# MLP's first product in two halves of 512 moving columns, from the fourth piece on

## The chip, the cores and the metric

The kernel runs on one core of one Trainium2 chip. The metric is device time in microseconds, the median of several runs.

## The reference

Two layers over 256 tokens of width 1024. The first mixes by neighbourhood attention and latent attention, the second by dilated windows. Each layer ends in a squared-ReLU MLP with 4096 inner features. That MLP is what the change touches:

```python
def rms_norm(x, g):
    xf = x.astype(jnp.float32)
    y = xf * lax.rsqrt(jnp.mean(xf * xf, axis=-1, keepdims=True) + RMS_EPS)
    return (y * g.astype(jnp.float32)).astype(x.dtype)

def sq_relu_mlp(xn, w1, w2):
    return jnp.square(jax.nn.relu(xn @ w1)) @ w2

def reference(...):
    for layer in range(DEPTH):
        xn = rms_norm(x, norm_mix[layer])
        ...
        x = x + sq_relu_mlp(rms_norm(x, norm_mlp[layer]), mlp_w1[layer], mlp_w2[layer])
    return rms_norm(x, norm_final)
```

## The kernel before

Every product of float32 numbers is made of three products of fp32r numbers. A number is split into a high part, a cast by ScalarE (ACT), and a low part, number minus high part, by VectorE (DVE). `split` (lines 217 to 219) does it, and `mm3` (lines 221 to 224) issues the three matmuls: high by high, high by low, low by high. So weights `raw` that come from memory become `whi` and `wlo`, tokens become `xx` (both parts in one tile, `xT[:, k, 0]` high and `xT[:, k, 1]` low, which lie next to each other), and inner features `h` become `hh` and `hl`.

An MLP works in 16 pieces of 256 inner features. `up(j, pu)` makes piece j of the first product: for each half f of 128 features and each of 8 slices k of the width, three matmuls with 128 weight columns as the stationary and 256 tokens as the moving operand, into one PSUM bank of 512 columns, 256 for each half. Then ACT takes relu (line 386) and the square `h` (line 388). The second product uses seven block products in place of eight (`SEVEN`, after Strassen) for pieces 0 to 13: three subtractions on DVE (lines 393 to 395) make the operands from `h`, and `down(j, m)` issues 7 times three matmuls of 512 columns into banks `m`. Pieces 14 and 15 use eight plain block products, made at the end by `last`.

The order in the program is up(0), up(1), up(2), down(0), up(3), down(1), up(4), down(2) and so on to up(15), down(13). From up(3) on, `up` writes the bank `m["C22"]`, which no other product uses before `last("C22")`. I call up(j + 2) and the down(j) behind it a round. Banks of PSUM have the names `w` and `acc` in the profile; C22 is one of the four `w`.

Weights come on SyncE's DMA queue, 1 MB for a piece of w1 and 0.75 MB for three blocks of w2. For the seven products, sums of blocks of w2 are needed too: a base block is loaded into `sum` (line 140), copied by ACT (line 154), and two more blocks are added to it by an accumulating DMA that GpSimd issues (line 155). DVE adds further sums (`raw` line 189, `every` line 190), and ACT and DVE split them into `sumh` and `suml`. `weight()` hands out the next weight tiles and, ahead of them, issues loads and splits. There are three buffers for `whi`/`wlo`, four for `raw`, three for `sum`, two for `sumh`/`suml`, one for `h`.

A scheduler sets the order of instructions on each engine from their dependencies and priorities; `tc.high_priority` moves what stands in it forward. Each engine then works through its list in that order.

In the second MLP (`finish`), `beside` is `tokens_first`: while down(2), down(4), down(6) and down(8) run, PE turns a quarter of the tokens (four transposes, line 502) in the bank C22, and ACT copies it out (line 503).

The odd layer's `qk_steps` (lines 955, 956, 962, 963) already multiplies both parts of the tokens as one moving operand of 512 columns: the high weights by both parts into 512 columns of a bank, then the low weights by the high parts into columns 256 to 511. ACT copies the upper half of the bank to `low`, and DVE adds it to the lower half.

Of the kernel before, what the change touches and what calls it, by code (L numbers as in the profile page):

```python
# [22 lines left out]
ALU = mybir.AluOpType  # L23
# [3 lines left out]
P = 128  # L27
D = 1024
KT = D // P
T = 256  # L30
# [19 lines left out]
def trunk(ctx, tc, a, out):  # L50
# [9 lines left out]
    def scratch(shape, name):  # L60

        n = int(np.prod(shape))
        v = work.tile([P, 512], F32, tag="scratch", name=name, bufs=12)[:, :n]
        if len(shape) == 2:
            v = v.rearrange("p (a b) -> p a b", b=shape[1])
        return v
# [298 lines left out]

    EIGHT = {"P2": ((1, 0), (0, 1)), "Q3": ((1, 3), (0, 2)), "C22": ((3, 3), (2, 2)), "Q4": ((3, 0), (2, 1))}

    def mlp(mp, xT, s, apart=(), beside=lambda j, p: None):

        hs = {}
        quarters = [act.tile([P, KT // 2, T], F32R, tag="quarter", name="hh", bufs=4) for _ in range(3)]

        def up(j, pu):
            w = weight()

            ranges = [range(4), range(4, 6), range(6, 8)] if j == 0 else [range(8)]
            for ks in ranges:
                for f in range(2):  # L380
                    for k in ks:
                        c = slice(k * 256 + f * P, k * 256 + f * P + P)
                        mm3(pu[:, (1 - f) * T:(2 - f) * T], w[0][:, c], w[1][:, c], xT[:, k, 0, :], xT[:, k, 1, :],
                            k == 0 and (f == 0 or j > 0), k == KT - 1 and (f == 1 or j > 0))
            r = scratch([512], "relu")
            nc.scalar.activation(r, pu, AF.Relu)
            h = mp.tile([P, 8, P], F32, tag="h", name="h", bufs=1)
            nc.scalar.activation(h[:, 4:8, :].rearrange("p (t f) n -> p f t n", f=2), r.rearrange("p (f t n) -> p f t n", f=2, t=2), AF.Square)
            hh = quarters[j % 3].rearrange("p a (b n) -> p (a b) n", n=P)
            hl = mp.tile([P, 7, P], F32R, tag="hl", name="hl", bufs=3)  # L390
            hs[j] = hh, hl
            if j < 14:
                nc.vector.tensor_tensor(h[:, 2:4, :], h[:, 7:8, :].broadcast_to([P, 2, P]), h[:, 5:7, :], op=ALU.subtract)
                nc.vector.tensor_tensor(h[:, 1, :], h[:, 5, :], h[:, 3, :], op=ALU.subtract)
                nc.vector.tensor_tensor(h[:, 0, :], h[:, 4, :], h[:, 1, :], op=ALU.subtract)  # L395
                split(hh[:, 0:7, :], hl, h[:, 0:7, :])
            else:
                split(hh[:, 0:4, :], hl[:, 0:4, :], h[:, 4:8, :])

        def down(j, m):  # L400
            wh, wl = weight()
            hh, hl = hs[j]
            first = j == 0
            for n, i, b in SEVEN:
                end = j == 13 and (n not in EIGHT or n in apart)
                mm3(m[n], hh[:, i, :], hl[:, i, :], wh[b], wl[b], first, end)
                if n == "Q3":
                    beside(j, m["C22"])

        for j in range(3):  # L410
            up(j, bank("w"))
        inv = inverse_columns(s)
        m = {n: bank("w" if n in ("P1", "P2", "Q6", "C22") else "acc") for n in ("P1", "P2", "Q6", "C22", "Q7", "Q5", "Q3", "Q4")}
        for j in range(14):
            if j:
                up(j + 2, m["C22"])
            down(j, m)
        tail = {j: weight() for j in (14, 15)}

        def last(n, o=None, c=slice(0, BLK)):  # L420
            o = m[n] if o is None else o
            new = n == "C22" or n in apart
            for j, w in tail.items():
                for i, (at, b) in enumerate(EIGHT[n]):
                    wh, wl = (z[:, b * BLK + c.start:b * BLK + c.stop] for z in w)
                    mm3(o, hs[j][0][:, at, :], hs[j][1][:, at, :], wh, wl, new and (j, i) == (14, 0), (j, i) == (15, 1))

        return m, last, inv
# [56 lines left out]
    def finish(mp, xT, s):  # L485

        state["pool"] = mp
        HALF = [slice(0, 512), slice(512, D)]
        xt = []
        v = {}  # L490

        def tokens_first(j, pt):

            if j % 2 == 0 and 2 <= j < 10:
                t, h = divmod(j // 2 - 1, 2)
                if not xt:

                    spare = act.tile([P, KT // 2, T], F32R, tag="quarter", name="xt0", bufs=4)
                    xt.extend((spare.bitcast(F32).rearrange("p k n -> p (k n)"), mp.tile([P, D], F32, name="xt1")))
                v[t, h] = xt[t][:, HALF[h]]  # L500
                for k in range(4):
                    nc.tensor.transpose(pt[:, k * P:(k + 1) * P], x[:, 4 * h + k, tok(t)], ident)
                nc.scalar.copy(v[t, h], pt)

        m, last, inv = mlp(mp, xT, s, ("Q4",), tokens_first)
        i0, i1 = (column(inv, t) for t in range(NT))
        g = [scratch([512], "gain") for _ in HALF]
        for h, cs in enumerate(HALF):
            nc.sync.dma_start(g[h], a["norm_final"][cs].partition_broadcast(P))

        def square_sum(z, o):
            nc.scalar.activation(scratch([z.shape[-1]], "junk"), z, AF.Square, scale=D ** -0.5, accum_out=o)

        def sub(o, y, z, op=ALU.subtract):
            nc.vector.tensor_tensor(o, y, z, op=op)
            return o

        sc = lambda n: scratch([512], n)
        last("P2")
        p = sc("p")  # L520
        nc.scalar.copy(p, m["P1"])
        onto_tokens(v[0, 0], p, i0, v[0, 0])
        both = sub(sc("both"), m["Q6"], p)
        c12 = sub(p, m["Q5"], both, ALU.add)
        c21 = sub(both, m["Q7"], both, ALU.add)
        onto_tokens(v[0, 1], c12, i0, v[0, 1])
        onto_tokens(v[0, 0], m["P2"], i0, v[0, 0])
        c22 = sub(sc("c22"), m["Q5"], c21, ALU.add)
        last("Q3")
        c21 = sub(c21, m["Q4"], c21)  # L530
        onto_tokens(v[1, 1], c22, i1, v[1, 1])
        onto_tokens(v[0, 1], m["Q3"], i0, v[0, 1])
        onto_tokens(v[1, 0], c21, i1, v[1, 0])
        last("C22")


        ss = work.tile([P, 4], F32, tag="ssf", name="ss")
        for h in range(2):
            square_sum(v[0, h], ss[:, h:h + 1])
            sub(v[0, h], v[0, h], g[h], ALU.mult)  # L540
        nc.vector.tensor_scalar(ss[:, 2:3], ss[:, 0:1], ss[:, 1:2], EPS, ALU.add, ALU.add)
        r = rsqrt(ss[:, 2:3], "x")
        onto_tokens(v[1, 1], m["C22"], i1, v[1, 1])
        for h, cs in enumerate(HALF):
            y = sc("y")
            nc.scalar.activation(y, v[0, h], AF.Copy, scale=r)
            nc.sync.dma_start(out[0:P, cs], y)


        ss = work.tile([P, 4], F32, tag="ssf", name="ss")  # L550
        xg = [sc("xg") for _ in range(2)]
        square_sum(v[1, 1], ss[:, 0:1])
        sub(xg[1], v[1, 1], g[1], ALU.mult)
        for i, c in enumerate((slice(0, 256), slice(256, 512))):
            o = bank("w")[:, 0:256]
            last("Q4", o, c)
            z = v[1, 0][:, c]
            onto_tokens(z, o, i1, z)
            if i == 0:
                square_sum(z, ss[:, 1:2])  # L560
                sub(xg[0][:, c], z, g[0][:, c], ALU.mult)
            else:
                nc.vector.tensor_scalar(ss[:, 2:3], ss[:, 0:1], ss[:, 1:2], EPS, ALU.add, ALU.add)
                nc.vector.tensor_tensor_reduce(out=scratch([256], "junk"), in0=z, in1=z, op0=ALU.mult, op1=ALU.add,
                                               scale=1.0 / D, scalar=ss[:, 2:3], accum_out=ss[:, 3:4])
        r = rsqrt(ss[:, 3:4], "x")

        parts_of = [(xg[h][:, 256 * i:256 * i + 256], out[P:T, 512 * h + 256 * i:512 * h + 256 * i + 256]) for h in (1, 0) for i in range(2)]
        nc.scalar.activation(parts_of[0][0], parts_of[0][0], AF.Copy, scale=r)
        for z, _ in parts_of[1:3]:  # L570
            nc.vector.tensor_scalar(z, z, r, None, ALU.mult)
        nc.vector.scalar_tensor_tensor(parts_of[3][0], v[1, 0][:, 256:512], r, g[0][:, 256:512], ALU.mult, ALU.mult)
        for n, (z, o) in enumerate(parts_of):
            (nc.scalar, nc.sync, nc.sync, nc.scalar)[n].dma_start(o, z)
# [609 lines left out]
```

## Time and profile before

| | |
|---|---|
| median of 3 runs | 731.53 us (731.29 to 731.69) |
| profiled execution: time / span | 731.99 us / 730.2 us |
| granted TensorE clock, mean | 0.997 |
| first MLP, first relu to last relu | 122.4 to 269.7 us of the span |
| second MLP, first relu to last relu | 558.1 to 708.8 us of the span |
| copies like `low` (128x256, ACT, line 962) | 0.366 us, 42 of them |
| adds like `z` (128x256, DVE, line 963) | 0.416 us, 42 of them |

The profile gives for each instruction its start in the span, its duration, its engine, its line and its tiles (out<-in). PE is TensorE's matmuls and PEld its weight loads, DVE is VectorE, ACT ScalarE, POOL GpSimd, SP SyncE. Matmuls overlap: a duration is longer than the distance to the next start.

### The profile page before, as it was taken

What the parts mean: (1) busy time and instruction counts of PE and PEld (TensorE: products, weight loads), DVE (VectorE), ACT (ScalarE), POOL (GpSimd) and SP (SyncE); (2) the same over time, 40 slices, a digit from 0 to 9 for tenths busy, and PEclk for the clock granted to TensorE, in tenths of its full rate; (3) what the DMA queues carried; (4) which work ended last, traced back from release to release, by engine and by line L of the source; (5) the groups of instructions that cost most, each with busy time, mean ns of one, the idle gap of its engine ahead of it and who ended that gap; (6) DMA issues with size and microseconds to landing.
All of it is one profiled execution on the core that took longest, in us unless ns stands there. A gap on an engine that the chain in (4) does not pass through costs nothing.

```text
span 730.2 us, 13797 instructions
## 1 busy us (share of the span) xinstructions
PE 721.5 (99%) x5234; PEld 661.0 (91%) x5234; DVE 614.0 (84%) x1179; ACT 531.5 (73%) x1001; POOL 40.7 (6%) x51
## 2 busy tenths in 40 slices
PE   9999999999999999999999999999999999999996
PEld 6998999999999998989899899998999999999995
DVE  5887859989999959889777888778759999989857
ACT  6778977876877856877676766867658788767752
POOL 0100011110111000000000000000002110011000
PEclk9999999999999999999999999999999999999998
DMA  8774339699899644664655556455658899998611
GB/s 312 273 255 150 116 121 227 213 263 261 255 273 268 199 150 162 222 217 154 213 174 186 170 187 202 167 187 202 207 186 209 249 275 239 254 247 227 208 52 59
DMA packets 38499, 149.56 MB, mean 205 GB/s; under 512 B 5152, under 2 KB 7200, under 8 KB 29344
## 3 DMA queue, kind: packets, MB, share of 16 engines
q1 hardware_dynamic: 30384, 133.71, 52.9%
q0 software_dynamic: 7616, 14.68, 11.8%
q8 instruction: 41, 0.67, 0.4%
q10 hardware_dynamic: 432, 0.28, 0.1%
q14 instruction: 26, 0.21, 0.1%
HBM read 142.10 MB, written 1.05 MB: 196 GB/s over the span
## 4 chain that ended last, share of the span: by engine, by line
PE 67%; issue 12%; DVE 10%; DMA 7%; ACT 3%; POOL 0%; SPq 0%; POOLq 0%; DVEq 0%; ACTq 0%
PE acc L955 11%; PE acc L222 8%; PE acc L223 8%; PE acc L224 8%; DMA sum<-in_w 6%; PE w L223 6%; PE w L222 6%; PE w L224 6%; PE acc L956 5%; DVE wlo L219 4%; PE w L231 1%; PE w L1032 1%; DVE suml L219 1%; ACT whi L218 1%; PE acc L1047 1%
## 5 line engine op out<-in xcount | busy, mean ns | idle before, releaser
L219 DVE TENSOR_TENSOR wlo<-raw,whi 128x512 fp32r<-128x512 f32 (+3 forms) x360 | 295.7, 844 | 56.5 <-ACT whi L218 56.3
L218 ACT CAST whi<-raw 128x512 fp32r<-128x512 f32 (+3 forms) x360 | 253.1, 746 | 75.4 <-PE w L223 47.8
L223 PE MATMUL w<-xx,whi 128*128 128x256 f32 x528 | 149.6, 284 | 0.3 <-DVE xx L259 0.3
L224 PE MATMUL w<-xx,wlo 128*128 128x256 f32 x528 | 149.3, 283 | 0.0
L222 PE MATMUL w<-xx,whi 128*128 128x256 f32 x528 | 148.8, 283 | 0.0
L955 PE MATMUL acc<-xx,whi 128*128 128x512 f32 x336 | 122.0, 404 | 0.0
L223 PEld LDWEIGHTS w<-xx,whi 128*128 128x128 f32 x528 | 101.1, 192 | 1.6 <-DVE xx L259 0.5
L222 PEld LDWEIGHTS w<-xx,whi 128*128 128x128 f32 x528 | 101.0, 192 | 1.1
L224 PEld LDWEIGHTS w<-xx,wlo 128*128 128x128 f32 x528 | 101.2, 192 | 0.0
L956 PE MATMUL acc<-xx,wlo 128*128 128x256 f32 x336 | 94.3, 281 | 0.0
L955 PEld LDWEIGHTS acc<-xx,whi 128*128 128x128 f32 x336 | 63.1, 188 | 14.2
L956 PEld LDWEIGHTS acc<-xx,wlo 128*128 128x128 f32 x336 | 63.5, 189 | 0.0
L222 PE MATMUL acc<-whi,xx 128*128 128x384 f32 (+2 forms) x160 | 55.8, 351 | 0.1
L223 PE MATMUL acc<-wlo,xx 128*128 128x384 f32 (+2 forms) x160 | 55.3, 345 | 0.2 <-DVE wlo L219 0.2
L224 PE MATMUL acc<-whi,xx 128*128 128x384 f32 (+2 forms) x160 | 54.9, 343 | 0.0
L155 POOL DMA_DIRECT2D sum<-in_w x28 | 30.9, 1137 | 215.1 <-ACT sum L154 154.9
L222 PE MATMUL w<-whi,hh 128*128 128x512 f32 (+1 forms) x108 | 42.1, 390 | 0.0
L223 PE MATMUL w<-wlo,hh 128*128 128x512 f32 (+1 forms) x108 | 41.5, 384 | 0.0
L224 PE MATMUL w<-whi,hl 128*128 128x512 f32 (+1 forms) x108 | 41.2, 382 | 0.0
L219 DVE TENSOR_TENSOR suml<-sum,sumh 128x1024 fp32r<-128x1024 f32 x28 | 34.2, 1220 | 4.9 <-ACT sumh L218 4.8
L218 ACT CAST hh<-h 128x896 fp32r<-128x896 f32 (+1 forms) x32 | 28.8, 901 | 6.7 <-DVE h L395 6.4
L219 DVE TENSOR_TENSOR hl<-h,hh 128x896 fp32r<-128x896 f32 (+1 forms) x32 | 33.2, 1036 | 0.1
(235 smaller groups left out, 1521.1 us busy)
## 6 DMA issues: line engine op xcount, KB each, us to landing
raw<-in_w SPq DMA_DIRECT2D x36, 1024.0 KB, 5.3
raw<-in_w_oqk SPq DMA_DIRECT2D x24, 1024.0 KB, 4.9
raw<-in_w SPq DMA_DIRECT2D x28, 768.0 KB, 4.5
sum<-in_w POOLq DMA_DIRECT2D x28, 512.0 KB, 8.7
raw<-in_w_ov SPq DMA_DIRECT2D x16, 768.0 KB, 4.4
sum<-in_w SPq DMA_DIRECT2D x28, 256.0 KB, 6.2
sw<-qk SPq DMA_DIRECT2D x84, 64.0 KB, 2.5
raw<-in_w_oe SPq DMA_DIRECT2D x4, 1024.0 KB, 6.6
```

What stands on the lines that cost most here:

```text
L155: nc.gpsimd.dma_start(sums, blocks[:, 0:3:2, :], accum_op=ALU.add)
L218: a = nc.scalar.copy(hi, src).ins
L219: return a, (eng or nc.vector).tensor_tensor(lo, src, hi.bitcast(F32), op=ALU.subtract).ins
L222: nc.tensor.matmul(o, sh, mh, start=first, stop=False)
L223: nc.tensor.matmul(o, sh, ml, start=False, stop=False)
L224: nc.tensor.matmul(o, sl, mh, start=False, stop=last)
L231: nc.tensor.matmul(o[j], y[pb, 0, ts], z[pb, 1, :], start=n == 0, stop=n == 2)
L955: nc.tensor.matmul(two(pq), wh[:, ws], xT[:, k], start=k == 0, stop=False)
L956: nc.tensor.matmul(pq[:, T:2 * T], wl[:, ws], xh[:, k, :], start=False, stop=k == KT - 1)
L1032: nc.tensor.transpose(pt[:, b * P:(b + 1) * P], pp[:, at:at + P], ident)
L1047: nc.tensor.matmul(pvo[cs, tok(i)], d["v0"][:, kk, cs], pts[j][:, kk, :], start=kk == 0, stop=False)
```

## The change

Pieces 0 to 2 stay as they are. From piece 3 on, `up` is replaced by two halves. Half f multiplies the high weights by both parts of the tokens (512 moving columns) and the low weights by the high parts (256 columns into the upper half of the same bank). That gives two matmuls for each slice k in place of three. ACT copies the upper half of the bank to `low` and DVE adds the lower half, into one half of a tile `z` in SBUF. Half 0 stands ahead of down(j), half 1 in the middle of it, behind P1, P2 and Q3. Relu and the rest (`features`) follow half 1 and read `z`. The transposes of tokens in the second MLP now come behind up(0), up(1) and up(2), each in a bank of its own.

```diff
+        def up_halves(j, o):
+            hold = {}
+            def half(f):
+                if f == 0:
+                    hold["w"], hold["z"] = weight(), scratch([512], "z")
+                w, z = hold["w"], hold["z"]
+                for k in range(KT):
+                    c = slice(k * 256 + f * P, k * 256 + f * P + P)
+                    nc.tensor.matmul(two(o), w[0][:, c], xT[:, k], start=k == 0, stop=False)
+                    nc.tensor.matmul(o[:, T:2 * T], w[1][:, c], xT[:, k, 0, :], start=False, stop=k == KT - 1)
+                low = scratch([T], "low")
+                with tc.high_priority(NORM_PRIO):
+                    nc.scalar.copy(low, o[:, T:2 * T])
+                    nc.vector.tensor_tensor(z[:, (1 - f) * T:(2 - f) * T], o[:, 0:T], low, op=ALU.add)
+                if f == 1:
+                    features(j, z)
+            return lambda: half(0), lambda: half(1)
+
+        def features(j, pu):
             r = scratch([512], "relu")
             nc.scalar.activation(r, pu, AF.Relu)
...
-        def down(j, m):
+        def down(j, m, between):
...
                 if n == "Q3":
-                    beside(j, m["C22"])
+                    between()
 
         for j in range(3):
             up(j, bank("w"))
+            beside(j)
...
         for j in range(14):
-            if j:
-                up(j + 2, m["C22"])
-            down(j, m)
+            first, second = up_halves(j + 2, m["C22"]) if j else (lambda: None,) * 2
+            first()
+            down(j, m, second)
...
-        def tokens_first(j, pt):
-            if j % 2 == 0 and 2 <= j < 10:
-                t, h = divmod(j // 2 - 1, 2)
+        def tokens_first(j):
+            for t, h in ([(0, 0)], [(0, 1), (1, 0)], [(1, 1)])[j]:
+                pt = bank("w")
```

The two matmuls of a half are lines 398 and 399 of the changed file, the copy is line 402, the add 403, relu 411, the square 413, the subtractions 418 to 420, the transposes 528.

DVE in the middle of the first MLP, one round before. Numbers behind names tell tiles apart; two `wlo` with one number belong to one weight tile.

```order
L219 TENSOR_TENSOR hl_2291<-h_2289,hh_1628 128x896
L189 TENSOR_TENSOR raw_2436<-sum_2345,raw_2436 128x512
L190 TENSOR_TENSOR every_2548<-raw_2436 128x512
L219 TENSOR_TENSOR wlo_2439<-raw_2328,whi_2438 128x1024 x2
L393 TENSOR_TENSOR h_2397<-h_2397 128x256
L219 TENSOR_TENSOR wlo_2516<-raw_2405,whi_2515 128x1024
L394 TENSOR_TENSOR h_2397<-h_2397 128x128
L219 TENSOR_TENSOR wlo_2516<-raw_2405,whi_2515 128x1024
L395 TENSOR_TENSOR h_2397<-h_2397 128x128
L219 TENSOR_TENSOR suml_2556<-sum_2345,sumh_2555 128x1024
L219 TENSOR_TENSOR suml_2556<-every_2548,sumh_2555 128x512
```

The same place of DVE now, from the add of half 1 to the add of the next half 0 and on:

```order
L403 TENSOR_TENSOR z_2410<-w_1858,low_2463 128x256
L219 TENSOR_TENSOR wlo_2493<-raw_2391,whi_2492 128x1024 x2
L219 TENSOR_TENSOR wlo_2532<-raw_2430,whi_2531 128x1024
L418 TENSOR_TENSOR h_2468<-h_2468 128x256
L219 TENSOR_TENSOR wlo_2532<-raw_2430,whi_2531 128x1024
L403 TENSOR_TENSOR z_2509<-w_1858,low_2526 128x256
L419 TENSOR_TENSOR h_2468<-h_2468 128x128
L190 TENSOR_TENSOR every_2593<-raw_2490 128x512
L420 TENSOR_TENSOR h_2468<-h_2468 128x128
L219 TENSOR_TENSOR suml_2601<-sum_2408,sumh_2600 128x1024
L219 TENSOR_TENSOR suml_2601<-every_2593,sumh_2600 128x512
L219 TENSOR_TENSOR hl_2470<-h_2468,hh_1630 128x896
```

Two adds that wait for PE by way of ACT now stand among the splits; the other instructions are the same.

ACT at that place before, from one relu to the next:

```order
L386 ACTIVATE relu_2503<-w_1858 128x512
L218 CAST whi_2546<-raw_2436 128x1024
L388 ACTIVATE h_2505<-relu_2503 128x2x2x128
L218 CAST whi_2623<-raw_2513 128x1024 x2
L154 COPY sum_2669<-sum_2669 128x512
L218 CAST sumh_2663<-sum_2453 128x1024
L218 CAST sumh_2663<-every_2656 128x512
L218 CAST hh_1630<-h_2505 128x896
L218 CAST whi_2654<-raw_2544 128x1024
```

ACT now, from the copy of half 1 on:

```order
L402 COPY low_2562<-w_1858 128x256
L218 CAST whi_2591<-raw_2490 128x1024
L218 CAST whi_2630<-raw_2529 128x1024
L411 ACTIVATE relu_2565<-z_2509 128x512
L218 CAST whi_2630<-raw_2529 128x1024
L413 ACTIVATE h_2567<-relu_2565 128x2x2x128
L218 CAST sumh_2699<-sum_2507 128x1024
L402 COPY low_2625<-w_1858 128x256
L154 COPY sum_2705<-sum_2705 128x512
L218 CAST sumh_2699<-every_2692 128x512
L218 CAST hh_1628<-h_2567 128x896
L218 CAST whi_2789<-raw_2688 128x1024
```

Relu no longer follows PE directly but stands one or two casts behind `low` and waits for `z`; the copy of the base block (line 154) went from ahead of `sumh` to behind the `low` of half 0.

PE at the start of the second MLP, in up(0), now:

```order
L222 MATMUL w<-xx,whi 128x256
L528 MATMUL w<-ident,x 128x128 x3
L223 MATMUL w<-xx,whi 128x256
L224 MATMUL w<-xx,wlo 128x256
L222 MATMUL w<-xx,whi 128x256
L528 MATMUL w<-ident,x 128x128
L223 MATMUL w<-xx,whi 128x256
```

Before, no transposes stand here, and this is a place of theirs, in down(2):

```order
L223 MATMUL acc<-wlo,hh 128x512
L224 MATMUL acc<-whi,hl 128x512
L502 MATMUL w<-ident,x 128x128 x4
L222 MATMUL w<-whi,hh 128x512
L223 MATMUL w<-wlo,hh 128x512
```

The first set went to where the matmul of line 223 needs the low part of the tokens, which DVE has still to make.

More of the change, by code (lines that the diff above doesn't have):

```diff
@@ L366, in trunk, with mlp @@
     EIGHT = {"P2": ((1, 0), (0, 1)), "Q3": ((1, 3), (0, 2)), "C22": ((3, 3), (2, 2)), "Q4": ((3, 0), (2, 1))}
-    def mlp(mp, xT, s, apart=(), beside=lambda j, p: None):
+    def mlp(mp, xT, s, apart=(), beside=lambda j: None):
         hs = {}
@@ L384, in up @@
                             k == 0 and (f == 0 or j > 0), k == KT - 1 and (f == 1 or j > 0))
+            features(j, pu)
+        def up_halves(j, o):
[16 more added lines that the diff above has]
+        def features(j, pu):
             r = scratch([512], "relu")
```

## The prediction

> **What bounds the kernel now.** I read the page's busy line first, then the stretches by round, then TensorE's own rows, then the two engines that feed it.
>
> ```profile
> PE 721.5 (99%) x5234; PEld 661.0 (91%) x5234; DVE 614.0 (84%) x1179; ACT 531.5 (73%) x1001; POOL 40.7 (6%) x51
> ```
>
> A busy share of 99% may hide short stalls, since ends of matmuls are modelled. So I take the distance between starts. The stretches below are rounds of the MLP (one piece of the first product, one of the second), cut at starts of relu; the columns are the length, busy time of PE, PEld, DVE, ACT and POOL, granted clock, DMA share and GB/s.
>
> ```profile
> 206.54:217.08 10.54, 10.54 (x70) 9.70 (x69) 10.36 (x14) 7.87 (x12) 1.09 (x1) 1.00 0.91 257
> 248.60:259.10 10.50, 10.50 (x71) 9.66 (x70) 8.22 (x10) 7.38 (x10) 0.00 (x0) 1.00 0.47 176
> 590.90:601.90 11.00, 11.00 (x75) 10.05 (x74) 11.00 (x16) 9.01 (x13) 1.09 (x1) 1.00 0.96 291
> ```
>
> PE fills each round at granted clock 1.00. DVE is nearly as full where a round prepares the sums of blocks (first and third row), not in the last rounds (second). The third round is longer by its four transposes.
>
> ```profile
> 157.49 0.28 PE L222 MATMUL w<-xx,whi 128*128 128x256 f32 x1
> 163.12 0.28 PE L224 MATMUL w<-xx,wlo 128*128 128x256 f32 x1
> 163.24 0.40 PE L222 MATMUL w<-whi,hh 128*128 128x512 f32 x1
> 168.03 0.28 PE L222 MATMUL w<-xx,whi 128*128 128x256 f32 x1
> ```
>
> First product: 163.24 − 157.49 = 5.75 us for 48 matmuls of 256 columns, 0.1198 each. Second product: 168.03 − 163.24 = 4.79 us for 21 of 512 columns, 0.228 each. Their sum is the round: PE issues without a stall, so the MLP lasts as long as its matmuls.
>
> **PE's term.** A pair (512 columns, then 256) takes the place of three matmuls of 256, which cost 0.359 us. The odd layer has such pairs:
>
> ```profile
> 324.79 0.40 PE L955 MATMUL acc<-xx,whi 128*128 128x512 f32 x1
> 325.85 0.40 PE L955 MATMUL acc<-xx,whi 128*128 128x512 f32 x1
> ...
> 401.44 0.39 PE L955 MATMUL acc<-xx,whi 128*128 128x512 f32 x1
> 402.48 0.39 PE L955 MATMUL acc<-xx,whi 128*128 128x512 f32 x1
> ```
>
> Three pairs take 1.06 us in the first place and 1.04 in the second: 0.353 and 0.347 each. I take 0.350, the middle. A piece has 16 of them: 16 × (0.359 − 0.350) = 0.15 us (0.10 to 0.20). There are 13 such pieces in each MLP, 26 in all: **−3.9 us** (−2.6 to −5.2). The round becomes 10.54 − 0.15 = 10.39.
>
> By the Trainium skill (TensorE: Matmul & The Clock Gate, Back-to-back issue gap) an isolated matmul's gap is N/2.4 + 2.5 ns, 109 ns at 256 columns and 216 at 512. One fewer matmul would then be worth 2.6 ns a pair, 1.1 us in all, an estimate from that page. The rows disagree: 120 and 228 ns, some 13 ns over the streaming time each, and that overhead is what the change saves.
>
> **What DVE and ACT get.** One round of DVE, from one hl to the next:
>
> ```profile
> 206.04 1.08 DVE L219 TENSOR_TENSOR hl<-h,hh 128x896 fp32r<-128x896 f32 x1
> 207.04 0.68 DVE L189 TENSOR_TENSOR raw<-sum,raw 128x512 f32<-128x512 f32 x1
> 207.76 0.69 DVE L190 TENSOR_TENSOR every<-raw 128x512 f32<-128x512 f32 x1
> 208.37 2.35 DVE L219 TENSOR_TENSOR wlo<-raw,whi 128x1024 fp32r<-128x1024 f32 x2
> 210.64 0.42 DVE L393 TENSOR_TENSOR h<-h 128x256 f32<-128x256 f32 x1
> 210.98 1.22 DVE L219 TENSOR_TENSOR wlo<-raw,whi 128x1024 fp32r<-128x1024 f32 x1
> 212.11 0.28 DVE L394 TENSOR_TENSOR h<-h 128x128 f32<-128x128 f32 x1
> ...
> 213.87 1.23 DVE L219 TENSOR_TENSOR suml<-sum,sumh 128x1024 fp32r<-128x1024 f32 x1
> 215.02 0.69 DVE L219 TENSOR_TENSOR suml<-every,sumh 128x512 fp32r<-128x512 f32 x1
> 215.62 1.09 DVE L219 TENSOR_TENSOR hl<-h,hh 128x896 fp32r<-128x896 f32 x1
> ...
> L962 ACT COPY low<-acc x42: 348/366/375, 317.0 to 512.3; 128x256 f32<-128x256 f32 x42
> L963 DVE TENSOR_TENSOR qk<-acc,low x42: 412/416/425, 317.5 to 513.1; 128x256 f32<-128x256 f32 x42
> ```
>
> 215.62 − 206.04 = 9.58 us without a real gap. The odd layer's add is the operation that the change puts in: 0.416 us, or 0.34 from start to start (the first h, as large: 210.64 to 210.98). Two per round make 9.58 + 0.68 = **10.26 of 10.39 us**. ACT gets two copies of 0.366 and has 10.54 − 7.87 = 2.67 us free. So throughput is kept, barely, and what decides is whether low and z come in time, because half 1 and the next half 0 write into the bank that they read.
>
> The cover: nine matmuls of the second product lie between halves 0 and 1, 9 × 0.228 = 2.05 us, and twelve between half 1 and the next half 0, 2.74. At the least an exchange takes 0.28 − 0.12 (the last matmul's end) + 0.37 + 0.42 = 0.95; with one cast of ACT just begun (0.94, next fence) 1.9. It fits if DVE comes to z on time. Both queues keep their order, so I walk one round with rows' start distances and the new order, t = 0 at the end of half 1:
>
> ```profile
> 206.47 0.59 ACT L386 ACTIVATE relu<-w 128x512 f32<-128x512 f32 x1
> 206.96 1.04 ACT L218 CAST whi<-raw 128x1024 fp32r<-128x1024 f32 x1
> 207.90 0.63 ACT L388 ACTIVATE h<-relu 128x512 f32<-128x512 f32 x1
> 208.43 1.99 ACT L218 CAST whi<-raw 128x1024 fp32r<-128x1024 f32 x2
> ...
> 212.27 0.62 ACT L154 COPY sum<-sum 128x512 f32<-128x512 f32 x1 [1.85 <-DMA sum<-in_w]
> ```
>
> ACT: low done at 0.6, a whi 1.55, another 2.5, relu 3.0, whi 3.95, h 4.5, sumh 5.45, then the low of half 0, whose matmuls end at 2.74 + 16 × 0.35/2 = 5.54. DVE: z done at 1.0, three wlo behind those casts by 5.1, the first h 5.5, suml or wlo 6.6, z of half 0 done at 7.0. Half 1 may start at 5.54 + 2.05 = 7.6. Then h, suml, h, raw, every, hl and a wlo follow (4.5 us): next z done at 11.9, that is 1.5 into the next round, where 2.74 is allowed. A DVE late by 0.5 finds fewer waits for casts and is back at the same place. So in a settled round I charge PE nothing; its cover is DVE's lead of 0.6 (before half 1) and 1.2 us (before half 0).
>
> Charges. In the first rounds of both MLPs DVE runs without a gap and comes late; before, a late DVE cost nothing there. I charge one late half in each MLP, between 0 and 1.14 (a wlo in front of z), 0.6 each: **+1.2 us** (0 to 4, if four halves). At the end, piece 15's hh and hl come later against its use: half 1, low, z, relu, h, hh with two casts of 0.95 and four smaller ones among them, an estimate of 5.6 us from these rows, against 24 matmuls that the new order of MLP0 puts first (5.5): **+0.2 us** (0 to 1). The weight buffer of a first-product piece is now freed at the end of half 1 and the second product's next weights are due 2.74 + 2.77 = 5.5 us later, where it was a whole round; the walk has them at 3.9 and 5.1, the second part due at 6.9: nothing. Relu reads SBUF and not a bank: nothing. The loads keep their number, and base loads wait as before:
>
> ```profile
> ACT sum L154 <- DMA sum<-in_w: 21.2, 10, 5.0
> ```
>
> That copy stood ahead of relu and now stands behind low of half 0, ahead of hh; it was ready 1.85 us late in front of an idle ACT and is asked for about as late: nothing.
>
> MLP1's transposes keep their number and move into its first three pieces; three of four sets cost PE there what they cost before. The first goes where PE now waits:
>
> ```profile
> 553.71 0.28 PE L224 MATMUL w<-xx,wlo 128*128 128x256 f32 x1
> 554.32 0.39 PE L223 MATMUL w<-xx,whi 128*128 128x256 f32 x1 [0.32 <-DVE xx L259]
> ...
> 591.94 0.60 PE L502 MATMUL w<-ident,x 128*128 128x128 f32 x4
> 592.29 0.48 PE L222 MATMUL w<-whi,hh 128*128 128x512 f32 x1
> 592.61 0.40 PE L223 MATMUL w<-wlo,hh 128*128 128x512 f32 x1
> ```
>
> A set costs 592.61 − 591.94 − 0.23 = 0.44 us; the wait is 0.61 − 0.24 = 0.37 of free time: **−0.3 us** (0 to −0.4). Their four copies on ACT come early, where relu and hh of piece 2 stand behind them; hl of that piece is due two rounds later.
>
> **Sum:** −3.9 − 0.3 + 1.2 + 0.2 = −2.8 us. The profiled execution took 731.99 (span 730.2 and 1.8 around it), 0.46 above the runs' median of 731.53. So the median becomes 731.53 − 2.8 = **728.7 us**.
>
> **Rivals.**
>
> *Slower: z of half 1 closes a loop.* Once that z ends later than 1.55 us after its half, ACT's relu waits for it, and DVE's next wlo and h wait for casts behind that relu. The loop is then z 0.34, relu 0.49, whi 0.94, h 0.53, whi 0.95, wlo 1.14, h 0.34, raw 0.72, z 0.34, h 0.20 (its row's 0.28 less the overlap of 0.08), every 0.61, h 0.20, suml 1.15 and 0.60, hl 1.0, wlo 1.14 = 10.7 us against 10.54 now. Some 22 rounds carry sums: 22 × 0.17 = 3.7; four light ones give back 0.6 and the transposes 0.3: 731.53 + 2.8 = 734.3. It decides from a z that is late by 0.5 us against my walk. For it speaks the first table (DVE 10.36 and 11.00); against it that relu stands in this place in part of the rounds only.
>
> *No change.* Pairs at 0.353 give −2.6 − 0.3, and four or five late halves of 0.6 take 2.7 back: 731.3. The skill's 2.6 ns a pair would end here too.
>
> *More.* Pairs at 0.347, no late half: −5.2 − 0.3 = 726.0. For it: those pairs stood in a stretch without neighbours' waits, as the MLP is.
>
> **How the numbers follow.** Forecast (about 726.8 to 730.0) 0.45, more 0.10, no change 0.23, slower 0.22. From no change 0.2%, 1.46 us, is about what can be told: faster 0.55, same 0.23, slower 0.22. The range leaves out the outer part of both ends: 726.0 to 733.8, 8 in 10.
>
> **What would show it.** Pairs of L398 and L399 start 0.350 apart; a round lasts 10.39 in the middle of the MLP and the last rounds too. DVE rounds of 10.2 to 10.4 with idle time of some tenths before wlo. PE waits for z in a few early halves only. The forecast is wrong if PE has a wait for z in most rounds, if z ends more than 1.6 us after half 1, or if pairs cost 0.357.

## The result and the profile after

The changed kernel takes 739.14 us (median of four runs, 738.43 to 739.35), the kernel before beside it 731.61. The ratio is 1.0102, with an interval of 1.0085 to 1.012: slower by 7.5 us, where a gain of 2.8 was forecast, and outside the range. The profiled execution took 739.26 us, 737.4 of it the span. Two executions further down, one of the kernel before (1175.89 us) and one of the last experiment (752.65 us), ran at a lower granted clock than the others and are left out of the comparisons.

The page's busy line of the changed kernel, and below it three stretches, each one round from one half 0 to the next (length, PE, PEld, DVE, ACT, POOL, granted clock, DMA share, GB/s):

```profile
PE 722.9 (98%) x4818; PEld 636.7 (86%) x4818; DVE 628.3 (85%) x1231; ACT 548.0 (74%) x1053; POOL 41.0 (6%) x51
...
199.19:209.69 10.50, 10.50 (x54) 8.65 (x52) 10.23 (x16) 8.41 (x13) 1.09 (x1) 1.00 0.87 246
209.69:220.31 10.62, 10.62 (x54) 8.96 (x54) 10.40 (x15) 8.51 (x13) 1.09 (x1) 1.00 0.97 259
220.31:230.80 10.49, 10.49 (x54) 8.65 (x52) 10.22 (x16) 8.38 (x13) 1.09 (x1) 1.00 0.78 237
```

PE has 416 matmuls fewer, and its clock is 1.00 as before, yet a round is 10.5 to 10.6 us long, against 10.54 before and 10.39 forecast. So the settled rounds of the first MLP neither gained nor lost. TensorE's own rows show where the gain of a round went: first matmuls of the stretches of one round, second product, half 1, second product, next half 0.

```profile
212.62 0.40 PE L222 MATMUL w<-whi,hh 128*128 128x512 f32 x1
214.72 0.39 PE L398 MATMUL w<-xx,whi 128*128 128x512 f32 x1
217.53 0.40 PE L222 MATMUL w<-whi,hh 128*128 128x512 f32 x1
220.31 0.39 PE L398 MATMUL w<-xx,whi 128*128 128x512 f32 x1
```

Half 1 takes 217.53 − 214.72 = 2.81 us, so a pair 0.351, as forecast (0.350). But the second product, cut in two, takes 2.10 + 2.78 = 4.88 us, where its 21 matmuls took 4.79 in one stretch. The rest of the gain goes in every second round, where half 0 is 0.1 us longer (10.62 in the second stretch above), since its first pair waits that long for z.

The time is lost at single places. These rows of TensorE of the changed kernel carry the longest waits that the kernel before does not have (idle time and releaser in brackets); the first two lie where the odd layer begins, the third at the start of the second MLP, the last two in its rounds:

```profile
288.77 0.44 PE L222 MATMUL acc<-whi,xx 128*128 128x384 f32 x1 [0.41 <-ACT xx L258]
...
291.77 0.45 PE L223 MATMUL acc<-wlo,xx 128*128 128x384 f32 x1 [0.87 <-DVE wlo L219]
...
566.07 0.50 PE L222 MATMUL acc<-whi,hh 128*128 128x512 f32 x1 [0.98 <-ACT hh L218]
...
627.07 0.50 PE L398 MATMUL w<-xx,whi 128*128 128x512 f32 x1 [1.39 <-DVE z L403]
...
680.19 0.50 PE L398 MATMUL w<-xx,whi 128*128 128x512 f32 x1 [0.26 <-DVE z L403]
```

Only the last two are waits for z. The end of the kernel is late without a wait of PE. The kernel before: PE's first matmul behind piece 15, then the first step of DVE's closing chain, and GpSimd's that follows it:

```profile
707.71 0.40 PE L222 MATMUL w<-whi,hh 128*128 128x512 f32 x1
711.45 0.75 DVE L432 SCALAR_TENSOR_TENSOR xt<-p,ms,xt 128x512 f32<-128x512 f32 x1
721.03 0.58 POOL L249 TENSOR_TENSOR rstd<-ss,mhalf 128x1 f32<-128x1 f32 x1 [48.59 <-DVE ss L541]
```

and the changed kernel, at the same three places:

```profile
714.46 0.40 PE L222 MATMUL w<-whi,hh 128*128 128x512 f32 x1
719.02 0.75 DVE L458 SCALAR_TENSOR_TENSOR xt<-p,ms,xt 128x512 f32<-128x512 f32 x1 [0.70 <-ACT p L547]
728.31 0.58 POOL L249 TENSOR_TENSOR rstd<-ss,mhalf 128x1 f32<-128x1 f32 x1 [49.25 <-DVE ss L567]
```

In both, DVE works through its queue nearly without a gap from its row to GpSimd's: 9.58 us before, 9.29 after. The way there from the end of the first product is 3.74 us before and 4.56 after. It starts with the splitting of weights, as these rows of ACT and DVE show, before and then after:

```profile
707.79 1.05 ACT L218 CAST whi<-raw 128x1024 fp32r<-128x1024 f32 x1 [5.11 <-PE w L223]
708.87 1.23 DVE L219 TENSOR_TENSOR wlo<-raw,whi 128x1024 fp32r<-128x1024 f32 x1 [4.67 <-ACT whi L218]
```

```profile
714.54 1.05 ACT L218 CAST whi<-raw 128x1024 fp32r<-128x1024 f32 x1 [4.40 <-PE w L398]
715.62 1.23 DVE L219 TENSOR_TENSOR wlo<-raw,whi 128x1024 fp32r<-128x1024 f32 x1 [5.03 <-ACT whi L218]
```

ACT and DVE stand idle for four to five us until PE has used up the weights of piece 15, and only then split the next ones; low or relu, and with them the features, come behind that cast. So the end of the kernel hangs on the end of piece 15 by a chain of ACT and then DVE, some 22.5 us long (730.2 − 707.71), not on PE. And the change moved the end of piece 15 back: nine matmuls of the second product, 2.05 us, now stand ahead of its half 1. The distance from there to the end grew only from 22.5 to 737.4 − 714.46 = 22.9 us. Together 2.5 us. Other kernels bear this out: in the profile of every experiment below, that distance is 22.2 to 23.1 us, wherever piece 15 ends.

### The profile page after: what moved, and what is told of

The parts are those of the page before. It is cut to its first block, busy times and chain, and to the rows that moved or that the text cites. A ratio compares the mean times of both kernels' runs of the same rounds, so it can differ in the third digit from the quotient of the medians.

```text
span 737.4 us, 13044 instructions
## 1 busy us (share of the span) xinstructions
PE 722.9 (98%) x4818; PEld 636.7 (86%) x4818; DVE 628.3 (85%) x1231; ACT 548.0 (74%) x1053; POOL 41.0 (6%) x51
## 4 chain that ended last, share of the span: by engine, by line
PE 87%; DVE 5%; DMA 4%; ACT 2%; issue 1%; POOLq 0%; POOL 0%; SPq 0%; DVEq 0%; ACTq 0%
PE w L398 11%; PE acc L981 11%; PE acc L222 11%; PE acc L223 11%; PE acc L224 11%; PE w L399 6%; PE acc L982 5%; PE w L223 5%; PE w L222 5%; PE w L224 5%; DMA sum<-in_w 3%; PE w L231 1%; PE w L1058 1%; DVE wlo L219 1%; PE acc L1073 1%
## 5 line engine op out<-in xcount | busy, mean ns | idle before, releaser
L398 PE MATMUL w<-xx,whi 128*128 128x512 f32 x416 | 149.9, 400 | 1.7 <-DVE z L403 1.7
L399 PE MATMUL w<-xx,wlo 128*128 128x256 f32 x416 | 116.7, 280 | 0.0
L398 PEld LDWEIGHTS w<-xx,whi 128*128 128x128 f32 x416 | 78.1, 188 | 23.6 <-DVE z L403 4.7
L399 PEld LDWEIGHTS w<-xx,wlo 128*128 128x128 f32 x416 | 78.5, 189 | 1.5
L222 PE MATMUL acc<-sumh,hh 128*128 128x512 f32 x84 | 33.2, 395 | 0.0
L224 PE MATMUL acc<-sumh,hl 128*128 128x512 f32 x84 | 33.0, 393 | 0.0
```

Source lines behind the costliest of these rows:

```text
L222: nc.tensor.matmul(o, sh, mh, start=first, stop=False)
L224: nc.tensor.matmul(o, sl, mh, start=False, stop=last)
L398: nc.tensor.matmul(two(o), w[0][:, c], xT[:, k], start=k == 0, stop=False)
L399: nc.tensor.matmul(o[:, T:2 * T], w[1][:, c], xT[:, k, 0, :], start=False, stop=k == KT - 1)
```

## The experiments

Two theories stood against each other after this: that the *ends* of the MLPs lost (pieces 14 and 15 come out later, and a chain of ACT and DVE behind them waits for them), and that the *exchange* costs (low and z, 0.68 us of DVE a round). A third account was for the early transposes.

### Which pieces cost

Pieces 14 and 15 whole again, all else as changed:

```diff
-            first, second = up_halves(j + 2, m["C22"]) if j else (lambda: None,) * 2
+            first, second = (lambda: None,) * 2
+            if 0 < j < 12:
+                first, second = up_halves(j + 2, m["C22"])
+            elif j:
+                up(j + 2, m["C22"])
```

> The changed kernel, but pieces 14 and 15 of each MLP are made whole again, by the old up ahead of down(12) and down(13), relu from the bank. Theory of the late end (what stands behind an MLP's last pieces has lost its cover: half 1 of piece 15 ends nine matmuls later, and low, z, relu, square, casts follow): the 2.0 us between the first MLP and the odd layer's first products and some 2 of the 2.55 us behind the last half go, about 735. Theory of the exchange (each low and z, 0.68 us of DVE a round, is what costs): 4 of 26 pieces lose it, 4/26 of 7.5 = 1.2 us, about 738.

Measured 734.33 us (733.29 to 735.22), ratio to before 1.0035 (1.0022 to 1.0047): 4.8 us under the changed kernel. The counterpart is the kernel before with only pieces 14 and 15 in halves (`if j > 11` in the loop):

> The kernel before, with only pieces 14 and 15 of each MLP in halves with low and z; transposes and all else as before. Theory of the late end: nearly all of the 4.3 us of the two ends comes with these four pieces: 735 to 736. Rival (the ends are late because the rounds ahead of them ran late): 731.5 to 732.5.

Measured 736.48 us (736.20 to 737.26), ratio 1.0064 (1.0051 to 1.0078): 4.9 us over before. Four of 26 pieces carry 4.8 to 4.9 of the 7.5 us, put in or taken out. The waits at the start of the odd layer come back with them, here in TensorE's rows of that kernel:

```profile
290.22 0.44 PE L222 MATMUL acc<-whi,xx 128*128 128x384 f32 x1 [0.43 <-ACT xx L258]
...
293.21 0.45 PE L223 MATMUL acc<-wlo,xx 128*128 128x384 f32 x1 [0.87 <-DVE wlo L219]
```

The order on PE says why. Behind piece 15 of the first MLP, before, come 21 matmuls of down(13), then all 12 of P2's last products, then Q3's. In the changed kernel come 12 of down(13), then 6 of P2, 6 of Q3, one of C22, and so on in turns: hh of piece 15 is later, and the scheduler filled in what does not need it. P2 is complete later, and with it begins DVE's work on the new tokens (lines 432 before, 458 after: y from the banks):

```profile
276.42 2.07 DVE L432 SCALAR_TENSOR_TENSOR y<-w,ms,y 128x512 f32<-128x512 f32 x3 [1.48 <-PE w L224]
```

```profile
277.94 2.07 DVE L458 SCALAR_TENSOR_TENSOR y<-w,ms,y 128x512 f32<-128x512 f32 x3 [1.35 <-PE w L224]
```

1.52 us later, and the tokens `xx` of the odd layer with it. As at the end of the kernel, the delay of piece 15 passes through whole: from the first matmul behind it to the first of the second MLP the profile has 550.34 − 268.64 = 281.70 us before and 551.88 − 270.26 = 281.62 now, though nine matmuls fewer lie between.

For the settled rounds, halves in pieces 3 to 13 of the first MLP alone, the second MLP as before:

> The kernel before, with halves in pieces 3 to 13 of the first MLP alone; the second MLP and its transposes as before. This is what the change is worth in settled rounds. By the rounds of the profile (10.51 against 10.54, some 0.1 us late first pairs in every second one): 11 pieces at -0.03 to +0.03, 731.2 to 731.9. Forecast's term: 11 at 0.15, 729.9. Rival (each exchange costs 0.1 or more): 732.7 or more.

Measured 731.49 us (731.13 to 732.17, eleven runs), ratio 0.9997 (0.9988 to 1.0005). Neither the forecast's 1.6 us of gain nor a cost: eleven halved pieces are worth nothing that can be measured.

### The transposes

The kernel before with only the transposes moved (`beside(j)` behind `up(j, bank("w"))` for j below 3, each in a bank of its own):

> The kernel before, with only the transposes of the second MLP moved behind up(0), up(1) and up(2), in banks of their own, as in the changed kernel. Forecast's term: -0.3, about 731.3. Rival (the early copies on ACT push back relu, square and hh of the first pieces, and with them carry the 0.9 us net that the start of the second MLP lost): about 732.5, with a PE wait for hh or wlo in the first second-product pieces.

Measured 732.82 us (732.09 to 734.22, eleven runs), ratio 1.0017 (1.0008 to 1.0026): +1.3, the rival's side. TensorE's row at the first second-product piece:

```profile
564.64 0.50 PE L222 MATMUL acc<-whi,hh 128*128 128x512 f32 x1 [1.39 <-ACT hh L218]
```

ACT's cast of that hh, in the kernel before and in this one:

```profile
563.60 0.94 ACT L218 CAST hh<-h 128x896 fp32r<-128x896 f32 x1
```

```profile
563.65 0.94 ACT L218 CAST hh<-h 128x896 fp32r<-128x896 f32 x1
```

hh comes no later than before. But before, PE asked for it at 568.69, behind all of up(2); now the scheduler put the first three matmuls of down(0) ahead of up(2), and PE asks at 564.64 − 1.39 = 563.25, more than five microseconds earlier. The same wait is in the changed kernel at 566.07.

### The exchange, the pairs and the place

The halves made by the old three matmuls, without low and z:

```diff
-                    nc.tensor.matmul(two(o), w[0][:, c], xT[:, k], start=k == 0, stop=False)
-                    nc.tensor.matmul(o[:, T:2 * T], w[1][:, c], xT[:, k, 0, :], start=False, stop=k == KT - 1)
-                low = ...
+                    mm3(o[:, (1 - f) * T:(2 - f) * T], w[0][:, c], w[1][:, c], xT[:, k, 0, :], xT[:, k, 1, :], k == 0, k == KT - 1)
```

> The changed kernel with its order of halves, but each half is made by the old three matmuls of 256 columns into its half of the bank, and relu reads the bank: no pair, no low, no z. Theory of the late end: the place of the halves alone costs, some 1.5 to 2 us at each end of the two MLPs and 0.9 at the second start: about 735 to 736. Theory of the exchange: without low and z nothing waits: 731.6 plus at most 26 more switches between widths at 0.04 = 1.0, 731.6 to 732.7.

Measured 735.63 us (735.24 to 736.13), ratio 1.0055 (1.0041 to 1.0068). 1.3 of its 4.1 us are the transposes'; the place of the halves alone costs the other 2.8, though no engine has got any more to do. So the place alone can explain a good half of the 4.8 us; what low and z add to it comes on top. Without DVE's add, low copied straight into z:

```diff
-                    nc.scalar.copy(low, o[:, T:2 * T])
-                    nc.vector.tensor_tensor(z[:, (1 - f) * T:(2 - f) * T], o[:, 0:T], low, op=ALU.add)
+                    nc.scalar.copy(z[:, (1 - f) * T:(2 - f) * T], o[:, T:2 * T])
```

> The changed kernel without the add on DVE: ACT copies the upper half of the bank into z (the lower half of the bank, the high by high part of one half's moving columns, is left out). DVE gets the 0.68 us a round back, ACT keeps a copy, PE's matmuls stay. Theory of the exchange on a full DVE: the rounds' 2.25 us go and most of the ends: 732 to 734. Theory of the late end: each chain is shorter by one z, 0.4 us: about 737.

Measured 735.51 us (734.77 to 736.30), ratio 1.0053 (1.0040 to 1.0066), between the two expectations: the add is worth 3.6 us. Its trace has no wait for z left; the wait for hh at the second MLP's start stays.

What the pairs are worth by themselves: whole pieces in their old place, 16 pairs each:

```diff
+            if j > 2:
+                ranges = []
+                for f in range(2):
+                    for k in range(KT):
+                        c = slice(k * 256 + f * P, k * 256 + f * P + P)
+                        nc.tensor.matmul(two(pu), w[0][:, c], xT[:, k], start=k == 0, stop=False)
+                        nc.tensor.matmul(pu[:, T:2 * T], w[1][:, c], xT[:, k, 0, :], start=False, stop=k == KT - 1)
```

> The kernel before with pieces 3 to 15 still whole and in their old place, but as 16 pairs of 512 and 256 columns into the one bank (half 1 overwrites half 0, whose features are left out; the upper half is not added). No low, no z, no further switch, transposes as before. This is PE's term by itself. Forecast's term: 0.15 a piece, -3.9, about 727.6. By the halves of the changed kernel (2.81 against 2.875 us): 0.13 a piece, -3.4, about 728.2. Rival (what a pair saves is lost again behind it, since the first matmuls of 512 columns after a switch come 0.2335 apart): -1, about 730.5.

Measured 728.20 us (727.80 to 729.07), ratio 0.9953 (0.9940 to 0.9965): −3.4 us. PE's term was there to be had. And pairs in halves, without low and z (`features(j, o)` behind half 1):

> The changed kernel, with its halves of pairs in their places and its early transposes, but without low and z: relu reads the bank after half 1 (half 0's features are overwritten, the upper half is not added). Against the halves of three matmuls (735.63) it differs by the pairs alone. If a pair saves in this order what its row says: 735.6 - 3.4 = 732.2. Rival (the saving goes in the switches): 735.

Measured 734.92 us (734.02 to 735.65), ratio 1.0043 (1.0030 to 1.0055). Against halves of three matmuls the pairs save 0.7 us, not 3.4; the intervals of the two ratios overlap, so 0.7 is not sure to differ from nothing. One round each of whole pairs, of halves of three and of halves of pairs:

```profile
199.29:209.71 10.42, 10.42 (x54) 8.84 (x53) 8.80 (x12) 7.14 (x10) 1.09 (x1) 1.00 0.99 267
```

```profile
196.46:207.02 10.56, 10.56 (x71) 9.70 (x70) 9.27 (x13) 7.79 (x10) 1.09 (x1) 1.00 0.92 254
```

```profile
196.47:206.98 10.51, 10.51 (x56) 8.84 (x55) 9.09 (x12) 7.79 (x10) 1.09 (x1) 1.00 0.91 248
```

Cutting the second product costs 0.02 with halves of three (10.56 against 10.54) and 0.09 with halves of pairs (10.51 against 10.42). The exchange adds the 0.1 us by which half 0 comes late in every second round.

### Attempts to mend it

Last two pieces whole; in the second MLP the transposes at their old place and pieces 4, 6, 8 and 10 whole, since they need the bank between two pieces:

```diff
-    m, last, inv = mlp(mp, xT, s, ("Q4",), tokens_first)
+    m, last, inv = mlp(mp, xT, s, ("Q4",), tokens_first, (4, 6, 8, 10, 14, 15))
...
+            if j and j + 2 not in whole:
+                first, second = up_halves(j + 2, m["C22"])
```

> The changed kernel with the two things mended that cost: pieces 14 and 15 of both MLPs whole, and in the second MLP the transposes at their old place, with pieces 4, 6, 8 and 10 whole there (so halves in pieces 3 to 13 of the first MLP and in seven of the second). If the late end and the early transposes are the whole loss: 731.5 with the pairs' gain of 18 pieces at 0.04 to 0.13, 729.2 to 730.8. Rival (each exchange costs on a full DVE, in settled rounds too): 732.5 or more.

Measured 733.43 us (732.46 to 734.45, nine runs), ratio 1.0024 (1.0015 to 1.0034). Against 731.49 with the same halves in the first MLP alone, the second MLP loses some 1.9 us in seven halved pieces, where the first loses nothing in eleven. To take load off DVE, one of its sums went to GpSimd (`nc.gpsimd.tensor_tensor(every, ...)`), in the changed and in the mended kernel:

> The changed kernel, with one of the two sums of blocks (every) added on GpSimd, which is 6% busy, in place of DVE: DVE gets 0.61 us a round back, nearly what low and z cost it (0.68). Full DVE: the waits for z inside the second MLP (1.55 and 0.43 us) go and the end of each MLP comes a little earlier, as without the add: 736 to 737. Rival (GpSimd is slow at it, every is late for sumh, and the wait moves there): 739 or more.

> The mended kernel (pieces 14 and 15 whole, in the second MLP pieces 4, 6, 8 and 10 whole and the transposes at their old place), with every added on GpSimd. If the full DVE holds the 1.8 us that were left there: 731 to 732; with pairs' gain of 18 pieces on top 730.5. Rival (what was left there has another cause, or GpSimd is late): 733 or more.

Measured 753.38 us (ratio 1.0301, 1.0276 to 1.0325) and 745.98 us (1.0196, 1.0182 to 1.0210): on the side of the rivals, and far above the figures that they named. GpSimd's row of the first, and DVE's hl, min, median and longest, in it and in the changed kernel:

```profile
L190 POOL TENSOR_TENSOR every<-raw 128x512 f32<-128x512 f32 x28 | 58.1, 2074 | 71.6 <-DVE raw L189 54.7 <-ACT h L413 7.8 <-ACT xt L529 6.5
...
L219 DVE TENSOR_TENSOR hl<-h,hh x32: 682/1089/2195, 132.1 to 735.3; 128x896 fp32r<-128x896 f32 x28, 128x512 fp32r<-128x512 f32 x4
```

```profile
L219 DVE TENSOR_TENSOR hl<-h,hh x32: 682/1084/1093, 128.3 to 719.7; 128x896 fp32r<-128x896 f32 x28, 128x512 fp32r<-128x512 f32 x4
```

GpSimd needs 2.07 us on average (1.28 at the least) for what DVE does in 0.68, and DVE's own subtractions last up to 2.2 us in place of 1.1. By the Trainium skill (SBUF — State Buffer, SBUF: two separate sides) GpSimd and a DVE operation with two SBUF inputs take a shared pair of ports as an exclusive lock, for a whole instruction; these rows agree, since some hl last up to 1.1 us longer beside GpSimd's additions, and none does without them.

Last, the wait for z at 627.07 in the changed kernel. On ACT and then DVE ahead of it:

```profile
623.94 0.62 ACT L154 COPY sum<-sum 128x512 f32<-128x512 f32 x1 [1.77 <-DMA sum<-in_w]
624.46 0.63 ACT L413 ACTIVATE h<-relu 128x512 f32<-128x512 f32 x1
...
625.12 0.43 DVE L418 TENSOR_TENSOR h<-h 128x256 f32<-128x256 f32 x1 [1.80 <-ACT h L413]
625.46 1.22 DVE L219 TENSOR_TENSOR suml<-sum,sumh 128x1024 fp32r<-128x1024 f32 x1
626.60 0.41 DVE L403 TENSOR_TENSOR z<-w,low 128x256 f32<-128x256 f32 x1
```

A base copy waits for its load, the square h stands behind it on ACT, DVE's first subtraction waits for h, and suml and z stand behind that. So the copy went to GpSimd in all pieces (`nc.gpsimd.tensor_copy` in line 154):

> The changed kernel, but the copy of the base block into the second half of sum (line 154) always runs on GpSimd, which is idle there, and no longer stands in ACT's queue, where it waits for its load with the square h and the next low behind it (1.77 us at 623.9 in the second MLP). Theory of the copy in the queue: the waits of half 1 for z inside the second MLP (1.55 and 0.43 us) go, 737 to 737.5; the early transposes (1.3) and the last two pieces (4.8) stay. Rival (those waits come from DVE's full queue alone): 738.5 to 739.5. Third (GpSimd's copies slow DVE, as its additions did): 740 or more.

> The mended kernel (last two pieces whole, old transposes and pieces 4, 6, 8 and 10 whole in the second MLP), with the copies of the base blocks on GpSimd. If the copy in ACT's queue holds what was left there: 733.4 - 0.9 (its longest wait for z) or better, 731.5 to 732.5. Rival (DVE's queue, where suml and hl stand ahead of z): 733 to 734.

Measured 739.83 us (738.93 to 743.10, ratio 1.0115, 1.0095 to 1.0135) and 740.81 us (740.19 to 742.22, three executions, ratio 1.0127, 1.0107 to 1.0147). In the changed kernel PE's waits for z fell as the theory said; the lines of waits of that kernel and, below, of the changed one:

```profile
PE w L398 <- DVE z L403: 0.2, 1, 0.2
```

```profile
PE w L398 <- DVE z L403: 1.7, 2, 1.4
```

but the time did not: the wait for hh at the second MLP's start went from 0.98 to 1.54 us, and the copies on GpSimd have a price of their own, as the third theory of the expectation had it. DVE's first subtraction of each piece (min, median and longest) in that kernel and, below, in the changed one:

```profile
L418 DVE TENSOR_TENSOR h<-h x28: 408/418/832, 123.7 to 700.9; 128x256 f32<-128x256 f32 x28
```

```profile
L418 DVE TENSOR_TENSOR h<-h x28: 414/418/427, 124.1 to 698.8; 128x256 f32<-128x256 f32 x28
```

In that kernel 21 instructions of DVE last at least 15% and 0.08 us longer than the median of their kind, 6.9 us in sum, and each of them overlaps a copy on GpSimd; in the changed kernel there are 2, with 0.7 us. In the mended kernel a new wait for z of 3.71 us arose; ahead of that z, DVE stood idle for 3.05 us before a sum of blocks (line 189). So the copy in ACT's queue made the two waits, but what they cost in time these two runs do not show, since the cure slows DVE.

## Why the prediction was wrong, point by point

**PE's term, −3.9.** The price of a pair was right: 0.351 in the changed kernel, and −3.4 us with whole pieces. That is 8 ns saved on each, so not the whole of the 13 ns that the prediction calls a matmul's overhead. The step that failed is "The round becomes 10.54 − 0.15 = 10.39": it kept the second product at 4.79 us though the change cuts it in two. Cut, it takes 4.88, which takes back 0.09 of the 0.13 us, and with 0.1 us for a late half 0 in every second round the gain is gone (first MLP alone: ratio 0.9997). By the issue gap of the Trainium skill (TensorE: Matmul & The Clock Gate, Back-to-back issue gap) whole pairs would have been worth 1.0 us (2.5 ns for each of 416; the prediction has 2.6 and 1.1), an estimate; the run gave three times that, and the measurement decides.

**DVE's and ACT's walk, nothing a settled round.** The charge nearly held in the first MLP, whose PE waits for z 0.1 us in every second round, but the walk did not. It had z done 1.5 us into the next round. Counted from the first matmul behind half 1, the changed kernel has 1.9 us in some rounds of the first MLP and 2.7 in most of the others, where 2.78 lie before the next half 0. The cover is used up; the forecast's own sign of being wrong, a z later than 1.6 us, stands in every round of the first MLP. ACT, DVE and PE behind a half 1 that ends at 206.91:

```profile
206.99 1.05 ACT L218 CAST whi<-raw 128x1024 fp32r<-128x1024 f32 x1 [1.22 <-PE w L398]
207.95 0.36 ACT L402 COPY low<-w 128x256 f32<-128x256 f32 x1
...
208.08 1.23 DVE L219 TENSOR_TENSOR wlo<-raw,whi 128x1024 fp32r<-128x1024 f32 x1 [0.27 <-ACT whi L218]
209.22 0.42 DVE L403 TENSOR_TENSOR z<-w,low 128x256 f32<-128x256 f32 x1
...
209.69 0.50 PE L398 MATMUL w<-xx,whi 128*128 128x512 f32 x1
```

A cast of weights waits until half 1 frees their buffer, so it becomes ready together with low and stands ahead of it, and where DVE's `wlo` of these weights stands ahead of z, z ends at 209.64 and half 0 starts at once. In the second MLP even that did not hold, see below.

**The end, +0.2.** This is the step that decided the sign. I counted matmuls against the time of hh and hl, so I asked whether PE would wait. At the end of an MLP PE's matmuls do not set the time: a chain of ACT and DVE does, and it starts where piece 15's first product ends. The nine matmuls ahead of half 1 were put down as cover, but there they are delay. And I named one end, where there are two: at the first MLP's the odd layer's tokens come late in the same way. Measured: 4.8 to 4.9 us for both.

**The transposes, −0.3.** Measured +1.3 us. The filled wait was real, but the order around it was read at one place only: the first matmuls of down(0) came ahead of up(2), where hh was not ready.

**One late half for each MLP, +1.2.** The profiled execution has none in the first MLP and two in the second (1.39 and 0.26 us of waits in the rows). **The base copy, nothing:** wrong as a wait, since it made the longer one of these; what it costs in time is not shown. **Weight buffers, nothing:** no row of PE in a round waits for them, but ACT's cast does (1.22 us in the rows above), and low and z behind it pay; at the end of the kernel the chain starts with the same wait. **Relu from SBUF, nothing:** no row of a round shows a wait of relu for z.

**The rivals.** The slower rival was right in sign and wrong in mechanism and size: its condition, a z later than 1.55 us, was met in every round of the first MLP, yet there is no loop of z at 10.7 us a round, settled rounds are 10.5 to 10.6. The other two, no change (731.3) and more (726.0), put no more on the ends than the forecast did and were missed as well.

**What is left open.** 4.8 for the last pieces and 1.3 for the transposes make 6.1 of 7.5 us. By elimination the other 1.4 lie in the rounds of the second MLP: 734.33 − 732.82 = 1.5 is what halves in pieces 3 to 13 of both MLPs add to the early transposes, and those of the first add nothing. This rest is loosely known, since executions with pieces 14 and 15 whole differ by 2 us among themselves (733.29 to 735.22). Waits for z are there, and DVE's add is worth 3.6 us in all (its time and its place in the chains together), so DVE's full queue is the likeliest cause; but the kernel that took out the two longest waits slowed DVE elsewhere, and the runs do not settle it.

No kernel here that computes the whole result beats the one before. To keep the 3.4 us of whole pairs, half 1 would need a bank of its own, and in the rounds only C22 is free; the upper halves would still have to be added, and what would be left of the gain no run shows.

## What to carry to other kernels

Before work is moved later, ask for the last piece separately: in the middle of a loop what stands ahead of it is cover, at the end it is delay, and what bounds there may be a chain of other engines, even one that starts with a weight buffer. A saving per matmul is to be checked against the stretches beside it, which may take it back when they are cut. And where a scheduler sets the order, read its order at the start and the end of the phase, not in the middle alone.

## What the runs showed of the hardware

Matmuls of 512 columns come slower at first, and longer so behind pairs. In the first MLP, by mean distance of starts, halves of three matmuls are followed by some five at 0.233 us and then 0.227; halves of pairs by some nine at 0.233. Whole pairs, 32 matmuls long, are followed by 21 in 4.79 us, as before. The granted clock is 1.00 in all of them; what makes the difference was not found. An addition of 128x512 on GpSimd took 2.07 us on average beside a busy DVE, and stretched single DVE instructions from 1.1 to 2.2. Copies of 128x512 on GpSimd stretched DVE's subtraction of 128x256 from 0.42 to 0.83.
